# A two-layer decoder trunk on one core: a 128-token linear-attention core, part of the modulation sums taken later, and the first block's expert routing moved behind the first expert layer

## The chip, the core and the metric

The kernel runs on one core of a Trainium2 chip. The core has a matrix engine (PE, TensorE), a vector engine (DVE), a scalar engine (ACT), GpSimd (POOL), which here only gathers rows, and SyncE (SP), which issues almost all other DMAs. Each engine executes its own queue in order. The metric is device time in microseconds (us) of one execution.

## The reference, cut to what matters

512 tokens of width 1024 pass two layers; each layer is an attention and a PEER expert mixer, and each of these is preceded by an RMSNorm with shift and scale and followed by a gate that come from a conditioning vector c.

```python
mod = silu(c) @ mod_w[l] + mod_b[l]              # per layer: sh1, sc1, g1, sh2, sc2, g2, 1024 wide each
# layer 0: gated linear attention, 4 heads, dk 128, dv 256, in chunks of 64 tokens (8 chunks)
b = cumsum(log_a)                                # inside a chunk
scores = tril((q * exp(b)) @ (k * exp(-b)).T);   o = scores @ v + (q * exp(b)) @ state
state = exp(b_last) * state + (k * exp(b_last - b)).T @ v
# layer 1: shared K/V from the output of layer 0, window attention, 16 heads, sinks
# PEER in both layers: q = h @ w_q (8 heads x 2 halves x 128); s = q half @ subkeys (128 keys)
v1,i1 = top_k(s1,16); v2,i2 = top_k(s2,16); cs,ci = top_k(v1[:,None]+v2[None,:],16)
e = i1*128 + i2 of the winners; g = softmax(cs);  y = sum (g * gelu(h . u[e])) * v[e]
```

## The kernel before

Tokens stand in four blocks of 128. Blocks 1 to 3 get the expert mixer densely: `dense` goes over 128 slabs of 128 experts, multiplies every slab with the 384 tokens and weights the result by a routed table. Block 0 gets it by gathering its 128 chosen rows of u and of v per token (`gather_back`), row by row on POOL and DVE while the dense loop of the same layer runs on PE.

**Order of the work.** `gla` first computes norms, projections and decays of all tokens, with PE busy; `gemv` sums modulation vectors beside it: for each of 512 columns (a chunk) four loads of 512 KB, eight DVE operations (L129, L131), and four one-column matmuls (L137). A second loop in `gla` then goes over the four blocks: per head scores (L406), a masked copy (L408), and twice, for either 64-token half, scores times V (L412), q times the state (L413), k times V (L415) and the state's update (L416); then a norm (L148 to L152, L420), the output product with `gla_wo` (L435), and `fin0`, which normalizes the block again and routes it. Routing is `route_front` (four chunks of 32 projection matmuls, L529, with 8 matmul records of key scores, L534, and a top-16 on DVE, L444 to L452), `route` (top-16 of sums, two table lookups, softmax, all DVE) and in `route_block` three transposes (L545). `dense(0)` follows: a prologue writes the routed tables (`routed`, L577 to L591) and computes the first 28 slabs (`act`, L605) ahead; the loop over 128 slabs then does `act` for a later slab (24 matmuls) and 18 matmuls of L639. After the gathered rows of block 0 are summed, `g_attn` does the shared K/V and attention of block 0 and `gather_front` and `gather_sel` route it for layer 1, between the matmuls of the dense loop. `swa_d` ends the dense layer (`dense_end`: gated additions L190, L191, then `modulate_T`), projects K, V and Q (L902), runs window attention per block (`swa_core`), the output product (L916), and routes blocks 1 to 3. `dense(1)` and the end follow.

**What sets the order.** The program is written through a scheduler: each instruction has a priority (lower goes first), `prio(base)` opens a counter at `base`, and an instruction goes into its engine's queue when a time simulation finds its inputs and its buffer ready. The bases are R0 (routing of layer 0), D0 (dense 0), G1 (block 0 in layer 1, just under D0), SW (the window attention stage), R1 (routing of layer 1), D1 and GG (gathers, last). `issue_after(x)` puts an instruction behind x on x's engine. Buffers with one tag are shared: `gw` holds four 4 KB rows on each partition for gathered rows and for `g_attn`'s weights. In `dense` the loads of u (L599), v (L624) and the routed table (L611) go through SP; POOL waits for a free `gw` buffer before each gather (L717).

Of the kernel before, what the change touches and what calls it, by code (L numbers as in the profile page):

```python
# [16 lines left out]
ALU = mybir.AluOpType  # L17
# [25 lines left out]
NA = 28  # L43
GSC = 2.0 ** 14
PACE = [[1.5] * 28 + [2.5] * 100, [1.5] * 28 + [2.25] * 100]
# [3 lines left out]
def kernel(ctx, tc, x, c_col, pos, mod_w, mod_b, norm_g, w_in, w_gl, w_g2, b_g2, gla_ng, gla_wo,  # L49
# [217 lines left out]
    def gla(mod, mod_first, mod_more, finish):  # L267
# [9 lines left out]
        dec = gq.tile([P, HG, S // CH], F32, name="dec")  # L277
# [11 lines left out]
        with tc.tile_pool(name="gla", bufs=1, reuse_waits="tile") as gp1, \  # L289
# [40 lines left out]
            nc.gpsimd.memset(maskf[0:64, 64:128], 0.0)  # L330
# [25 lines left out]
            for h in range(HG):  # L356
# [8 lines left out]
                nc.vector.tensor_copy(dec[:, h, :], az.rearrange("p (c t) -> p c t", t=CH)[:, :, CH - 1])  # L365
# [4 lines left out]
                nc.vector.tensor_tensor(dl, kt_[:, h, :], dl, op=ALU.mult)  # L370
                nc.scalar.activation(bT, bT, AF.Exp, scale=-1.0)
# [17 lines left out]
        with tc.tile_pool(name="gla2", bufs=1, reuse_waits="tile") as g2, \  # L389
# [9 lines left out]
            for half in range(2):  # L399
                bcast_half(env, mod[:, 16:24], half, gate[:, ts(half, 512)])  # L400
            for b in range(NB):
                O = g2.tile([P, D], F32, name="O")
                for h in range(HG):
                    po = ps_tile(env, "po")[:, :DV]
                    psc = mm_tile()
                    nc.tensor.matmul(psc[:, :P], kt_[:, h, ts(b, P)], qt[:, h, ts(b, P)], start=True, stop=True)  # L406
                    sc = scT[h % 2]
                    nc.vector.copy_predicated(sc, mask, psc[:, :P])  # L408
                    for i in range(2):
                        lo = b * P + i * CH  # L410
                        hs = slice(i * CH, (i + 1) * CH)
                        nc.tensor.matmul(po[hs, :], sc[hs, hs], V[hs, b, ts(h, DV)], start=True, stop=False)  # L412
                        nc.tensor.matmul(po[hs, :], qt[:, h, lo:lo + CH], st[:, h, :], start=False, stop=True)  # L413
                        pss = mm_tile()
                        nc.tensor.matmul(pss[:, :DV], kd[hs, b, h, :], V[hs, b, ts(h, DV)], start=True, stop=True)  # L415
                        nc.vector.scalar_tensor_tensor(st[:, h, :], st[:, h, :], dec[:, h, 2 * b + i:2 * b + i + 1],  # L416
                                                       pss[:, :DV], op0=ALU.mult, op1=ALU.add)
# [101 lines left out]
    def route_front(env, l, hT, rp):  # L519
# [3 lines left out]
        for ch in range(4):  # L523
            pq = ps_tile(env, "mm")
            for q in range(4):
                w = wpool.tile([P, KT, P], F32, tag=wtag, name="w", bufs=wbufs)
                nc.sync.dma_start(w, peer_wq[l, ch * 4 + q])
                for kt in range(KT):
                    nc.tensor.matmul(pq[:, ts(q, P)], w[:, kt, :], hT[:, kt, :], start=kt == 0, stop=kt == KT - 1)  # L529
            qq = env.big.tile([P, 512], F32, tag=env.qq, name="qq")  # L530
            nc.scalar.copy(qq, pq)
            psc = ps_tile(env, "sc")
            for q in range(4):
                nc.tensor.matmul(psc[:, ts(q, P)], qq[:, ts(q, P)], sk_sb[l][:, q % 2, :], start=True, stop=True)  # L534
            sc = env.tmp.tile([P, 512], F32, tag=env.t2k, name="scg", bufs=env.scb)
            nc.scalar.copy(sc, psc)
            topk16(rp, [(sc[:, ts(q, P)], v16[:, ch * 4 + q, :], i16[:, ch * 4 + q, :]) for q in range(4)], NK)
        return route(rp, v16, i16)

    def route_block(env, l, b, hT, rp):  # L540
        g, i1, i2 = route_front(env, l, hT, rp)
# [11 lines left out]
    def dense(l, yps):  # L553
        Y = []
        first = []
        wd = dram.tile([NG * P, NK * TG], F32, name=f"wd{l}", tag=f"wd{l}")
        by_slot = wd.rearrange("(g p) (m c) -> m p g c", p=P, c=SL * TG)
        banks = ("y0", "y1", "y2", "y4", "y5", "y3")
        with tc.tile_pool(name="dna", bufs=1, reuse_waits="tile") as da, \
# [84 lines left out]
            with tc.tile_pool(name="dno", bufs=1, reuse_waits="tile") as do_:  # L644
# [3 lines left out]
                for i in range(NG, NA):  # L648
                    act(i, ahead[:, i, :], ("pa", "pm")[i % 2])
# [480 lines left out]
```

## Time and profile before

| | us |
|---|---|
| median of three runs | 3280.8 |
| the three runs | 3267.9 to 3281.03 |
| the profiled execution | 3281.36 |
| its span, first to last instruction | 3279.7 |

| stretch of the span, us | what runs |
|---|---|
| 0 to 222 | norms, projections, decays; modulation sums beside |
| 222 to 432 | linear attention core and output product, block by block; routing begins |
| 432 to 573 | routing of blocks 1 to 3 |
| 573 to 742 | prologue of dense 0 |
| 742 to 1780.5 | loop of dense 0, with gathers, then block 0's layer-1 attention and routing |
| 1780.5 to 2160 | window attention stage and routing of blocks 1 to 3 |
| 2160 to 2310 | prologue of dense 1 |
| 2310 to 3279.7 | loop and end of dense 1 |

The profile is one execution. Busy times are sums over an engine's instructions; a row of a timeline gives start, duration, engine, line, operation, destination and sources with shapes, and in brackets the idle time before it and what ended that. A matmul in plain float32 stands in the trace as two records, so `x64` of L529 is one chunk of 32 matmuls; one in the rounded form of `dense` (L605, L639) is one record.

### The profile page before, as it was taken

To read this page: it belongs to the slowest core of one execution; us is meant where nothing else is said; L and a number is where in the kernel's file an instruction comes from. 1 tells how busy PE (TensorE), PEld (TensorE's weight loads), DVE (VectorE), ACT (ScalarE), POOL (GpSimd) and SP (SyncE) were. 2 spreads that over 40 slices of the span, in tenths; PEclk is the share of its full clock that TensorE was granted. 3 is DMA by queue.
4 is the path that set the end of the run, shared out by engine and by line. 5 is a ranking of instruction groups with operands and counts; after the bars stand their busy time and mean duration, and the time that the engine had idled before them with its cause. 6 is when DMAs were issued, how large, how long until landed. Compare 5 with 4: busy or idle time off the path is not lost.

```text
span 3279.7 us, 45577 instructions
## 1 busy us (share of the span) xinstructions
PE 3087.9 (94%) x16858; PEld 2633.6 (80%) x16858; DVE 2396.3 (73%) x4699; ACT 1282.9 (39%) x1991; POOL 610.3 (19%) x542
## 2 busy tenths in 40 slices
PE   6999985999999999999997889899899999999998
PEld 4765675998889999999876446899789999999997
DVE  7754699989777777777655344999877777777776
ACT  3422322653333333333662344256333333333333
POOL 0000000005333333333000000000433232223230
PEclk9989998999999999999998989999999999999999
DMA  7666675789889898898744225658998888888874
GB/s 238 229 243 237 237 261 169 261 283 345 307 311 317 291 321 311 301 322 287 239 143 145 84 77 193 213 200 294 329 343 311 300 278 305 276 302 303 272 265 154
DMA packets 264888, 844.44 MB, mean 257 GB/s; under 512 B 27844, under 2 KB 77380, under 8 KB 258520
## 3 DMA queue, kind: packets, MB, share of 16 engines
q1 hardware_dynamic: 190936, 573.06, 49.4%
q0 software_dynamic: 73728, 268.47, 24.3%
q8 instruction: 132, 2.16, 0.3%
q14 instruction: 92, 0.75, 0.1%
HBM read 784.27 MB, written 57.16 MB: 257 GB/s over the span
## 4 chain that ended last, share of the span: by engine, by line
PE 81%; DVE 10%; DMA 5%; ACT 2%; issue 1%; SPq 0%; DVEq 0%; ACTq 0%
PE pa L605 32%; PE Y L639 30%; PE ps_mm L529 3%; PE pm L590 3%; PE ps_m L902 2%; DMA v<-in_v_t 1%; PE ps_mm L435 1%; PE ps_mm L260 1%; PE ps_mm L261 1%; PE ps_mm L259 1%; PE ps_mm L916 1%; DMA w<-in_gla_wo 1%; PE ps_po L808 1%; DMA w<-in_mod_w 1%; DVE s L446 1%
## 5 line engine op out<-in xcount | busy, mean ns | idle before, releaser
L717 POOL DMA_INDIRECT gu<-in_peer_u,ei x256 | 314.8, 1230 | 1991.3 <-DVE gu L725 1192.1
L244 DVE TENSOR_TENSOR XL<-u,XH 128x1024 fp32r<-128x1024 f32 x256 | 313.2, 1224 | 351.7 <-PE pa L605 197.4
L639 PE MATMUL Y<-XH,WH 128*128 128x512 f32 x1536 | 480.4, 393 | 9.8 <-ACT WH L243 9.8
L639 PE MATMUL Y<-XH,WL 128*128 128x512 f32 x1536 | 478.5, 393 | 4.1 <-DVE WL L244 4.1
L639 PE MATMUL Y<-XL,WH 128*128 128x512 f32 x1536 | 478.5, 392 | 0.2
L243 ACT CAST XH<-u 128x1024 fp32r<-128x1024 f32 x256 | 269.1, 1052 | 432.1 <-PE pa L605 359.2
L605 PE MATMUL pa<-hH,XH 128*128 128x384 f32 x2048 | 412.4, 341 | 2.2 <-ACT XH L243 1.6
L243 ACT CAST XH<-v 128x1024 fp32r<-128x1024 f32 x256 | 268.8, 1050 | 363.4 <-PE Y L639 312.2
L605 PE MATMUL pa<-hL,XH 128*128 128x384 f32 x2048 | 404.9, 336 | 0.0
L717 POOL DMA_INDIRECT gu<-in_peer_v,ei x256 | 290.9, 1136 | 608.6 <-DVE yg L735 567.4
L605 PE MATMUL pa<-hH,XL 128*128 128x384 f32 x2048 | 401.5, 335 | 2.2 <-DVE XL L244 2.2
L244 DVE TENSOR_TENSOR XL<-v,XH 128x1024 fp32r<-128x1024 f32 x256 | 313.0, 1223 | 109.9 <-ACT XH L243 106.2
L605 PEld LDWEIGHTS pa<-hH,XH 128*128 128x128 f32 x2048 | 365.1, 188 | 20.4 <-ACT XH L243 1.8
L605 PEld LDWEIGHTS pa<-hH,XL 128*128 128x128 f32 x2048 | 358.2, 188 | 3.2 <-DVE XL L244 2.9
L605 PEld LDWEIGHTS pa<-hL,XH 128*128 128x128 f32 x2048 | 358.8, 188 | 1.6 <-issue 0.8
L639 PEld LDWEIGHTS Y<-XH,WL 128*128 128x128 f32 x1536 | 289.0, 188 | 67.4 <-DVE WL L244 5.4
L639 PEld LDWEIGHTS Y<-XL,WH 128*128 128x128 f32 x1536 | 289.0, 189 | 64.4 <-DVE XL L244 1.1
L639 PEld LDWEIGHTS Y<-XH,WH 128*128 128x128 f32 x1536 | 286.3, 189 | 58.3 <-ACT WH L243 11.0
L735 DVE SCALAR_TENSOR_TENSOR yg<-gu,a,yg 128x1024 f32<-128x1024 f32 x254 | 325.0, 1279 | 1.4
L725 DVE SCALAR_TENSOR_TENSOR gu<-gu,htg 128x1024 f32<-128x1024 f32 x256 | 308.4, 1219 | 1.8 <-DMA gu<-in_peer_u,ei 1.7
L243 ACT CAST WH<-g 128x384 fp32r<-128x384 f32 x256 | 131.6, 514 | 383.4 <-DVE g L627 267.5
L529 PE MATMUL ps_mm<-hTd,w 128*128 128x128 f32 x1792 | 223.9, 279 | 10.1 <-DMA w<-in_peer_wq 8.2
(312 smaller groups left out, 3633.1 us busy)
## 6 DMA issues: line engine op xcount, KB each, us to landing
u<-in_u_t SPq DMA_DIRECT2D x256, 512.0 KB, 5.5
v<-in_v_t SPq DMA_DIRECT2D x256, 512.0 KB, 5.2
w<-in_peer_wq SPq DMA_DIRECT2D x128, 512.0 KB, 4.2
w<-in_mod_w SPq DMA_DIRECT2D x96, 512.0 KB, 5.0
wd<-wt SPq DMA_DIRECT2D x48, 1024.0 KB, 6.1
wg<-wd SPq DMA_DIRECT2D x192, 256.0 KB, 9.7
w<-in_gla_wo SPq DMA_DIRECT2D x32, 512.0 KB, 5.0
w<-in_swa_wo SPq DMA_DIRECT2D x32, 512.0 KB, 4.4
```

What stands on the lines that cost most here:

```text
L243: nc.scalar.copy(H, src)
L244: eng.tensor_tensor(L, src, H.bitcast(F32), op=ALU.subtract)
L259: nc.tensor.matmul(out, ah, bh, start=kt == 0, stop=False)
L260: nc.tensor.matmul(out, ah, bl, start=False, stop=False)
L529: nc.tensor.matmul(pq[:, ts(q, P)], w[:, kt, :], hT[:, kt, :], start=kt == 0, stop=kt == KT - 1)
L590: nc.tensor.matmul(pm[:, t, :], o1[:, u, :, w], og[:, n, u, :, w], start=n == 0, stop=n == 1)
L605: nc.tensor.matmul(pa[:, :TD], uu[:, kt, :], hh[:, kt, :], start=n + kt == 0, stop=n == 2 and kt == KT - 1)
L639: nc.tensor.matmul(Y[b][h], a[:, ts(b, P)], vv[:, ts(h, 512)], start=i == 0 and a is WH and vv is VH, stop=i == NK - 1 and a is WL)
L717: nc.gpsimd.indirect_dma_start(out=u, out_offset=None, in_=table, in_offset=bass.IndirectOffsetOnAxis(ap=ei[:, i:i + 1], axis=0))
L725: nc.vector.scalar_tensor_tensor(u, u, 1.0, ht, op0=ALU.mult, op1=ALU.mult, accum_out=a[:, i:i + 1])
L735: nc.vector.scalar_tensor_tensor(y, u, a[:, i:i + 1], y, op0=ALU.mult, op1=ALU.add)
L902: nc.tensor.matmul(pqs[b], hTs[b][:, kt, :], w(kt), start=kt == 0, stop=kt == KT - 1)
```

## The change

Five parts. (1) In `gla` the core works on 128 tokens: the scores of a block are one 128x128 matmul plus one for the 64x64 corner between the halves (from `kx`, a copy of the decayed keys of the first half), the mask keeps the whole lower triangle, q is scaled for the second half once per block (`qs`), and each head then has one q-state matmul, one scores-V, one k-V and one state update. (2) Six of the twelve modulation chunks of layer 1 leave `gla`; `late_mod` sums them inside `gather_back(0)`, from step 40 of the dense loop, two DVE operations per second step, with their loads in `gw` buffers. (3) `route_front` gives its projections, score matmuls and copies a priority of their own (`base`), ahead of the top-16. (4) The layer-1 routing of block 0 leaves the stretch beside dense 0: its first projection chunk is placed behind the last matmul of dense 0, `modulate_T` behind that chunk, the rest into the window attention stage; buffers are listed in another order there, so that the tiles for XD and the weights lie elsewhere. The three transposes of a routed block are placed behind the second projection chunk of the next one. (5) Six `act` slabs of dense 1 go ahead of the routed tables.

```diff
-            nc.gpsimd.memset(maskf[0:64, 64:128], 0.0)
+                even = dl.rearrange("p (b c t) -> p b c t", c=2, t=CH)[:, :, 0, :]
+                nc.scalar.copy(kx[:, h], even)
+                nc.vector.tensor_tensor(even, even, dec[:, h, :, 1:2].to_broadcast([P, NB, CH]), op=ALU.mult)
...
+                nc.scalar.copy(qs[:, :, 0, :], q4[:, :, 0, :])
+                nc.vector.tensor_tensor(qs[:, :, 1, :], q4[:, :, 1, :],
+                                        dec[:, :, b, 0:1].to_broadcast([P, HG, CH]), op=ALU.mult)
...
+                    nc.tensor.matmul(psc[0:CH, CH:P], kx[:, h, b, :], qt[:, h, b * P + CH:(b + 1) * P], start=True,
+                                     stop=True)
                     sc = scT[h % 2]
                     nc.vector.copy_predicated(sc, mask, psc[:, :P])
-                    for i in range(2):
-                        lo = b * P + i * CH
-                        hs = slice(i * CH, (i + 1) * CH)
-                        nc.tensor.matmul(po[hs, :], sc[hs, hs], V[hs, b, ts(h, DV)], start=True, stop=False)
-                        nc.tensor.matmul(po[hs, :], qt[:, h, lo:lo + CH], st[:, h, :], start=False, stop=True)
-                        pss = mm_tile()
-                        nc.tensor.matmul(pss[:, :DV], kd[hs, b, h, :], V[hs, b, ts(h, DV)], start=True, stop=True)
-                        nc.vector.scalar_tensor_tensor(st[:, h, :], st[:, h, :], dec[:, h, 2 * b + i:2 * b + i + 1],
-                                                       pss[:, :DV], op0=ALU.mult, op1=ALU.add)
+                    nc.tensor.matmul(po, qs[:, h].rearrange("p c t -> p (c t)"), st[:, h, :], start=True, stop=False)
+                    nc.tensor.matmul(po, sc, V[:, b, ts(h, DV)], start=False, stop=True)
+                    pss = mm_tile()
+                    nc.tensor.matmul(pss[:, :DV], kd[:, b, h, :], V[:, b, ts(h, DV)], start=True, stop=True)
+                    nc.vector.scalar_tensor_tensor(st[:, h, :], st[:, h, :], decb[:, h, b:b + 1], pss[:, :DV],
+                                                   op0=ALU.mult, op1=ALU.add)
...
+            with prio(base):
+                pq = ps_tile(env, "mm0" if ch == 0 and "mm0" in env.psum else "mm")
...
+            yield mm
...
+                if l:
+                    with prio(R1 - 100_000):
+                        acts(NF)
                 for g in range(NG):
                     routed(g)
-                    act(g, ahead[:, g, :], ("pa", "pm")[g % 2])
+                    acts(max(done, g + 1 if not l else NF + (g + 1) * (NA - NF) // NG))
...
+    def late_mod(at, outs):
+        for n, ch in enumerate(range(6, 12)):
+            acc = gb.tile([P, 512], F32, tag="gacc", name="gacc")
+            for e in range(4):
+                w = gb.tile([P, 2, 512], F32, tag="gw", name="w", bufs=4)
+                nc.sync.dma_start(w, mod_w[1][ch][e // 2, :, 2 * (e % 2):2 * (e % 2) + 2, :])
+                with tc.issue_after(at[LATE + 2 * (4 * n + e)].ins):
...
+            with tc.high_priority(), tc.issue_after(outs[LATE + 8 * n + 9].ins):
...
...
+            for tag, n, bufs in (("Q", 512, 3), ("qT", 512, 3), ("SC", 1024, 4), ("pT", 1024, 4), ("h4k", 1024, 6),
+                                 ("w", 1024, 3), ("mx", 4, 4), ("es", 4, 4), ("nm", 4, 4), ("den", 4, 4)):
                 sp.tile([P, n], F32, tag=tag, name=tag, bufs=bufs)
             XD = xd_tiles(sp)
...
+            renv.psum = {"mm0": (psa, "pm", 1)}
+            sel = gather_sel(renv, 1, hT0, sr, rbase - 600_000)
+            with tc.issue_after(after.ins):
+                first = next(sel)
             preload_sqrt(sp)
+            def after_add(b):
+                with tc.issue_after(first.ins):
+                    modulate_T(env, XD[b], (Ak, Bk, hk[b]), (A, B, hq[b]))
+            dense_end(sp, 0, Y, XD, after_add)
...
+            with prio(rbase - 500_000):
+                sel = rest(sel)
...
+                gen = route_block(renv, 1, b, hT, sr, SW - 100_000)
                 with prio(rbase):
-                    route_block(renv, 1, b, hT, sr)
+                    for _ in range(2):
+                        mm = next(gen)
+                    with tc.issue_after(mm.ins):
+                        rest(tails.pop()) if tails else None
+                    for _ in range(3):
+                        next(gen)
+                tails.append(gen)
...
-            gemv(penv, mod_w[1], range(12), modb_sb[:, 1, :], m1)
+            gemv(penv, mod_w[1], range(6), modb_sb[:, 1, :], m1)
```

## Rows read from the trace of the kernel before

**Rows 1.** The page: busy time of each engine, and the chain's shares.

```profile
PE 3087.9 (94%) x16858; PEld 2633.6 (80%) x16858; DVE 2396.3 (73%) x4699; ACT 1282.9 (39%) x1991; POOL 610.3 (19%) x542
PE 81%; DVE 10%; DMA 5%; ACT 2%; issue 1%; SPq 0%; DVEq 0%; ACTq 0%
```

**Rows 2.** Busy time by stretch: PE, PEld, DVE, ACT, POOL, granted clock, DMA share, GB/s.

```profile
222.00:250.00 28.00, 26.18 (x83) 12.01 (x81) 10.36 (x24) 6.00 (x17) 0.00 (x0) 0.65 0.53 201
372.00:432.00 60.00, 55.16 (x327) 38.74 (x325) 43.91 (x207) 20.92 (x43) 0.00 (x0) 1.00 0.68 233
432.00:573.00 141.00, 97.23 (x801) 92.13 (x801) 128.02 (x738) 32.17 (x50) 3.91 (x4) 0.90 0.61 210
902.00:1230.00 328.00, 327.43 (x1658) 298.03 (x1657) 245.31 (x331) 122.26 (x159) 113.29 (x99) 1.00 0.88 310
1780.50:1807.00 26.50, 0.00 (x0) 0.00 (x0) 25.48 (x123) 9.46 (x10) 3.97 (x4) 0.55 0.47 164
1807.00:1866.00 59.00, 53.48 (x151) 25.25 (x152) 16.58 (x67) 20.78 (x49) 0.96 (x1) 0.94 0.26 91
1866.00:2044.00 178.00, 162.27 (x764) 97.97 (x763) 75.14 (x215) 79.88 (x203) 0.00 (x0) 0.95 0.36 120
2044.00:2160.00 116.00, 100.41 (x769) 96.47 (x768) 107.16 (x642) 39.69 (x52) 0.00 (x0) 0.99 0.59 196
2160.00:2310.00 150.00, 144.01 (x1307) 134.23 (x1305) 138.76 (x125) 84.45 (x146) 0.00 (x0) 1.00 0.74 272
```

**Rows 3.** Timeline of PE in the attention core, blocks 0 to 2.

```profile
233.36 1.11 PE L413 MATMUL ps_po<-st,qt 128*64 128x256 f32 x2
234.40 1.11 PE L412 MATMUL ps_po<-V,scT 64*64 64x256 f32 x2
...
271.52 0.65 PE L413 MATMUL ps_po<-st,qt 128*64 128x256 f32 x2
272.09 0.70 PE L415 MATMUL ps_mm<-V,kd 64*128 64x256 f32 x2
272.72 0.64 PE L412 MATMUL ps_po<-V,scT 64*64 64x256 f32 x2
...
371.74 0.71 PE L415 MATMUL ps_mm<-V,kd 64*128 64x256 f32 x4
```

**Rows 4.** The same timeline in block 3: full-array matmuls, one-column matmuls.

```profile
409.58 3.65 PE L435 MATMUL ps_mm<-w,oT 128*128 128x512 f32 x8
...
424.60 0.95 PE L137 MATMUL ps_tr<-ones,gacc 128*128 128x1 f32 x8
```

**Rows 5.** Stretches of L131 alone: DVE busy (instructions), clock, DMA share, GB/s.

```profile
432.00:573.00 141.00, 14.01 (x19) 0.90 0.61 210
```

**Rows 6.** Waits and DMA issues in 902 to 1240, loop of dense 0.

```profile
POOL gu L717 <- DVE gu L725: 159.8, 59, 7.3
u<-in_u_t SPq DMA_DIRECT2D x41, 512.0 KB, 6.2
```

**Rows 7.** Timeline of SP and ACT in one step of that loop.

```profile
1152.81 0.33 SPq L599 DMA_DIRECT2D u<-in_u_t  x1
1161.58 1.05 ACT L243 CAST XH<-u 128x1024 fp32r<-128x1024 f32 x1 [1.75 <-PE pa L605]
```

**Rows 8.** Timeline at the end of dense 0: PE, SP, DVE, ACT.

```profile
1746.20 7.41 PE L529 MATMUL ps_mm<-hTg,w 128*128 128x128 f32 x64
1754.34 1.16 PE L534 MATMUL ps_sc<-sk,qq 128*128 128x128 f32 x8
1780.89 1.38 SPq L672 DMA_DIRECT2D XD<-xs  x3
1801.18 0.68 DVE L190 TENSOR_TENSOR ga<-Y,gate 128x512 f32<-128x512 f32 x1
1807.06 1.11 PE L163 MATMUL ps_tr<-ident,xn 128*128 128x128 f32 x4 [26.57 <-ACT xn L159]
```

**Rows 9.** Line 605 in 2100 to 2166: ns min/median/max, first and last start.

```profile
L605 PE MATMUL pa<-hH,XH x56: 333/334/537, 2131.2 to 2162.5; 128*128 128x384 f32 x56
```

More of the change, by code (lines that the diff above doesn't have):

```diff
@@ L43 @@
 NA = 28
+NF = 6
 GSC = 2.0 ** 14
+LATE = 40
 PACE = [[1.5] * 28 + [2.5] * 100, [1.5] * 28 + [2.25] * 100]
@@ L703, in gather_sel, with gather_back, extra @@
         return ei, gk
-    def gather_back(l, at, ht, ei, gk):
+    def late_mod(at, outs):
[5 more added lines that the diff above has]
+                with tc.issue_after(at[LATE + 2 * (4 * n + e)].ins):
+                    if e == 0:
+                        nc.vector.tensor_scalar_mul(acc, w[:, 0, :], cs[:, 0:1])
+                    for k in range(e == 0, 2):
+                        nc.vector.scalar_tensor_tensor(acc, w[:, k, :], cs[:, 2 * e + k:2 * e + k + 1], acc, op0=ALU.mult,
+                                                       op1=ALU.add)
+                if e < 3:
+                    yield
+            with tc.high_priority(), tc.issue_after(outs[LATE + 8 * n + 9].ins):
+                col = ps_tile(genv, "tr")
+                for q in range(4):
+                    nc.tensor.matmul(col[:, q:q + 1], acc[:, ts(q, P)], ones1, start=True, stop=True)
+            nc.vector.tensor_tensor(m1[:, ts(ch, 4)], col[:, 0:4], modb_sb[:, 1, ts(ch, 4)], op=ALU.add)
+            if ch == 9:
+                cols["A4"] = mod_scale(m1[:, 32:40], ng_sb[:, 1, 1, :], "A4")
+            yield
+    def gather_back(l, at, outs, ht, ei, gk):
+        more = late_mod(at, outs) if l == 0 else iter(())
+        seen = set()
+        def extra(step):
+            if step >= LATE and step % 2 == 0 and step not in seen:
+                seen.add(step)
+                next(more, None)
         steps = []
@@ L722, in gather_back @@
         for i in range(NH * TOPK):
+            extra(steps[i])
             u = fetch(peer_u, i)
@@ L729, in gather_back @@
         for i in range(NH * TOPK):
+            extra(steps[NH * TOPK + i])
             u = fetch(peer_v, i)
@@ L735, in gather_back @@
                     nc.vector.scalar_tensor_tensor(y, u, a[:, i:i + 1], y, op0=ALU.mult, op1=ALU.add)
+        for _ in more:
+            pass
         gt = row("gt")
@@ L939, in swa_d @@
                         finish(b + 1)
+            with prio(rbase):
+                rest(tails.pop())
+            return sel
     co, sn = rope_tables()
```

115 lines of the change are left out of this document (71 added, 44 removed).

## The prediction

> **What bounds the kernel now.** I read the shares of busy time first, then the busy time by stretch, and only then timelines. PE is busy for 94% of the span and carries 81% of the chain [rows 1], so time comes back where PE idles, where PE does work that could be less, or where another engine holds the end of a stage. The stretches [rows 2] show which is which. In the attention core (222 to 432) PE is the full engine: 26.2 of 28 us in block 0, 55.2 of 60 in block 3, and in block 0 at a granted clock of 0.65, that is with a large part at 1.2 GHz. In 432 to 573 DVE is (128 of 141 us), PE has 44 us idle. In the loop of dense 0 PE idles 0.6 us in 328. Between the dense layers PE idles 26.5 us at a stretch, then 5.5, 15.7 and 15.6 us in three stretches of the attention and routing stage. In the prologue of dense 1 both are near full. All sums are made against the profiled execution, 3281.36 us (span 3279.7 and 1.7 around it); the median, 3280.8, lies 0.6 below.
>
> **1. The core.** Before, a head takes one full score matmul and six matmuls on half of the array. In a warm stretch an L413 holds PE for 0.57 us, and so does an L412; an L415 that stands alone, with 0.70 in its row, holds it for 0.63 [rows 3]. Two L415 next to each other (x4 records) stand there with 0.71 together: those on different halves of the rows do overlap. Of 32 L415 matmuls 10 pairs stand so and 12 alone, 22 x 0.63 = 13.9 us, 0.87 a head. A head costs 4 x 0.57 + 0.87 = 3.15 us beside its full score matmul. After, three full-array matmuls of 256 columns: L435 does 512 columns in 3.65 / 4 = 0.91 us [rows 4], so 0.46 each, 1.37 us; the corner matmul (64 columns, no row of its own) lies between a quarter of 0.46 and a whole half-array step, 0.12 to 0.57; I take 0.35, since it too is on half of the columns. Saved: 3.15 - 1.72 = 1.43 us a head; 12 heads 17.2 us. Block 0's four heads run at steps of 1.04 [rows 3], 1.8 times as long: 4 x 1.43 x 1.8 = 10.3. Together 27.5 us of PE, on the path, because PE is full there. Three of the six chunks that leave lie before 432: 3 x 0.9 us of L137 [rows 4] = 2.7 more. Against it, PE's 4.8 idle us of 60 in block 3 [rows 2], mostly waits for `gla_wo` loads, may grow, and the new copies (`kx`, `qs`, about 0.4 us each on ACT and DVE, which have 65% and 27% of the time free in block 3) can delay a first head: I give back 3. Block 3 is ready 27 us earlier; the bounds are 15 and 36.
> The Trainium skill ("TensorEngine Tiling (Array Packing)", Key Properties) says that different tiles execute weight loads and matmuls in parallel, which speaks against merging halves. The trace agrees for neighbouring L415 [rows 3]; L412 and L413 alternate and don't overlap. If all did, the old head would be as short as the new one and this term would be about 0: a rival below.
>
> **2. Sums that leave the routing tail.** In 432 to 573, 19 of L131 take 14.0 us of DVE [rows 5]; with their first products and additions 15.6. DVE is the full engine there, so the tail shortens by 15.6 to 125 us. Earlier projections (part 3 of the change) can only feed its 13 idle us. Bounds 8 and 28. The start of dense 0 moves by -27 - 15.6, about **-43**.
>
> **3. The sums in dense 0.** 24 one-column matmuls in a full PE: 6 chunks x 0.95 [rows 4] = +6. DVE gets about 36 us over 46 steps; it has a quarter free (245 of 328 [rows 2]). DMA gets 24 loads of 512 KB in 46 x 8.3 = 382 us, 33 GB/s on 310 at a share of 0.88: near full, not over. The point that can go wrong is SP: each load waits there for a `gw` buffer, and behind it stand u, v and table loads. A u load is issued at 1152.81, lands after 6.2 us and is read at 1161.58 [rows 6, 7]: 2.6 us of slack. POOL today waits for such buffers 2.7 us on average [rows 6], about that slack; so I take a few short stalls, +4. Bounds +6 and +25. **+10**.
>
> **4. Block 0's routing out of dense 0.** Four chunks of 7.2 us (the row's 7.41 less the overlap) and 1.1 us of scores [rows 8] leave a full PE: **-33**. `g_attn` itself stays.
>
> **5. The gap.** PE's 26.6 us gap [rows 8] is DVE finishing that routing: the first gated addition starts at 1801.18, 20.7 us after the last matmul, though XD was issued at 1780.89. After, DVE can start at once if XD is loaded early (its tile lies elsewhere), after some 6.5 us if not. From the first addition to the first transpose took 5.9 us. The placed chunk covers 7.4 us; its fourth weight load must wait for a buffer, so I count 8.5 and transposes then: 26.6 - 8.5 = **-18**. Bounds -10 (XD late) and -20. PE no longer stands still before the stage, whose clock is 0.94 and 0.95 [rows 2]; what that gives back is in the next bound.
>
> **6. What the moved work costs there.** Chunks 2 to 4 add 3 x 8.3 = 25 us of PE to a stage with 5.5 + 15.7 us idle up to 2044, in pieces between dependent steps; I let 10 go into idle time: +15. Their 42 us of DVE go into 42 + 103 idle us; each single operation is under 2 us, so the chain is delayed little. The six slabs moved ahead bring less than they look: seven slabs (56 records, 8 each) were already computed from 2131 on, beside the top-16 [rows 9]. They can fill some of the 15.6 us that PE idles in 2044 to 2160, but each costs DVE 1.22 us in a stretch where DVE is at 107 of 116: -5. **+10**, bounds -10 (idle time and clock pay for all) and +31 (nothing is hidden, and the forced order of projections holds up the attention of the next block).
>
> Sum: -43 + 10 - 33 - 18 + 10 = -74; 3281.4 - 74 = **3207**.
>
> **Rivals.** (a) *SP becomes the bound in dense 0*, the case on the slow side: SP waits for each `gw` buffer as long as POOL's longest wait today, 7.3 us [rows 6], instead of the mean. 7.3 - 2.6 = 4.7 us x 24 = 113 us on the PE loop instead of 4: 3207 + 109 = 3316. From 6.5 us of wait per load on (24 x 3.9 = 94 us against 74 + 4 saved, and 16 us for half a percent) the kernel is slower than before. For it: SP's queue is in order. Against it: the scheduler puts a load into the queue when it holds the buffer for free, and the weights of `g_attn` pass SP through `gw` already. 6%. (b) *The core gives nothing*: halves that overlap, or `gla_wo` loads that hold the blocks anyway: only the sums help, -18 instead of -43: 3232. Against it: the steps of 0.57 and 1.04 us [rows 3]. 10%. (c) *The stage takes back what dense 0 gave*: gap -10, moved work +31: 3236. For it: PE is at 90% there. 12%. (d) *All idle time is used*: tail -28, moved work -5: 3180. 7%. (e) *The parts eat each other*, core at its low bound, stalls at +25 and (c) together: about 3265, no change. 5%.
>
> **How the numbers follow.** The forecast, 3207 give or take 22, has 60%. The range that leaves out no more than 2 in 10 goes from just below (d) to above (c): 3165 to 3245. About 0.5%, 16 us, is what a measurement can tell from no change. Faster by more: forecast, b, c, d, 0.89; within: e, 0.05; slower: a, 0.06.
>
> **What would show it.** Right: L412 and L413 at full width, 16 of each, spaced under 0.5 us; the first slab of dense 0 some 43 us earlier; no L131 after the start of the tail; steps of the dense 0 loop still 8.3 us between 40 and 86; the last L639 of dense 0 followed within 1 us by 64 records of L529, and transposes 8 to 9 us behind; the time from that last L639 to the main loop of dense 1 some 8 us shorter than its 530. Wrong: steps of that loop over 8.5 us with SP waiting ahead of u; a DVE that is still full with routing when the core is done, so that the core's gain waits there; an attention stage over 20 us longer behind the transposes.

## The result and the profile after

The changed kernel takes 3245.8 us (median of four, 3238.72 to 3253.74); before, on the same chip, 3280.91 (3267.9 to 3286.62). The ratio is 0.9898, 95% interval 0.9876 to 0.992. The gain is 35 us where 74 were forecast, and the time lies 0.8 us above the top of the range. The profiled execution, 3253.74 us (span 3252.0), is the slowest of the four and gains 27.6; traces are compared on it, and one of the tables below shows how far a first stage moves without any change of its code.

The page of the kernel after, busy time of the engines and the shares of the chain, answers [rows 1]:

```profile
PE 3065.5 (94%) x16794; PEld 2641.4 (81%) x16794; DVE 2392.3 (74%) x4692; ACT 1276.0 (39%) x1997; POOL 628.2 (19%) x541
...
PE 65%; DMA 11%; DVE 10%; issue 8%; POOL 3%; ACT 2%; SPq 0%; POOLq 0%; DVEq 0%; ACTq 0%
```

PE is busy for 22 us less, so most of the 27.6 are work that went; its idle time hardly shrank, 187 us of the span against 192. DMA has 11% of the chain where it had 5%, and "issue" 8% where it had 1%.

Busy time by stretch of the kernel after answers [rows 2] (PE, PEld, DVE, ACT, POOL, granted clock, DMA share, GB/s). The stretches are: routing of blocks 1 to 3, part of the loop of dense 0, the gap, the window stage in four pieces (to the first window scores, to block 1's normalization, to block 3's, to the prologue), the prologue of dense 1.

```profile
386.00:530.00 144.00, 103.23 (x851) 98.25 (x851) 121.26 (x726) 39.86 (x62) 3.91 (x4) 0.90 0.55 187
860.00:1190.00 330.00, 324.14 (x1639) 294.10 (x1638) 256.12 (x357) 115.61 (x155) 122.46 (x94) 0.99 0.91 321
1723.00:1737.30 14.30, 9.00 (x65) 8.81 (x64) 8.38 (x13) 2.60 (x4) 0.00 (x0) 0.84 0.84 339
1737.30:1822.00 84.70, 79.29 (x382) 51.77 (x381) 43.84 (x284) 28.15 (x58) 0.00 (x0) 0.97 0.39 131
1822.00:1920.00 98.00, 84.04 (x348) 44.85 (x347) 51.98 (x124) 40.42 (x110) 3.74 (x4) 0.93 0.27 92
1920.00:2060.00 140.00, 123.89 (x746) 95.38 (x744) 92.48 (x505) 51.16 (x105) 0.00 (x0) 0.90 0.53 177
2060.00:2135.00 75.00, 67.33 (x464) 64.91 (x462) 51.70 (x251) 29.92 (x43) 0.00 (x0) 0.95 0.51 172
2135.00:2283.00 148.00, 138.76 (x1276) 129.36 (x1276) 136.04 (x121) 82.36 (x144) 0.00 (x0) 0.99 0.76 277
```

Two things are new against [rows 2]: the loop of dense 0 has 6 us of PE idle in 330 where it had 0.6 in 328, and the piece 1920 to 2060 has 16 us idle at a clock of 0.90, where [rows 2] have 0.94 to 0.99 in that stage.

**Where the time went.** The table reads each kernel's PE timeline at the same points: the first and the last slab matmul of a dense loop into Y (L639 before, L658 after), the first transposes behind dense 0, the first slab matmul of dense 1's loop. All in us; the experiments' rows are used further down.

| kernel | loop of dense 0 starts | loop | gap | first transposes to dense 1's loop | loop of dense 1 |
|---|---|---|---|---|---|
| before | 742.7 | 1037.8 | 26.6 | 505.6 | 951.9 |
| after | 698.7 | 1024.4 | 14.2 | 545.8 | 954.2 |
| change | -44.0 | -13.4 | -12.4 | +40.2 | +2.3 |
| forecast | -43 | -33 + 10 | -18 | +10 | 0 |
| e3, core alone | 714.0 | 1038.9 | 26.6 | 510.7 | 950.5 |
| e2, sums back in the prologue | 716.0 | 999.4 | 12.1 | 546.4 | 953.2 |
| e5, late sums without loads | 700.7 | 1009.2 | 13.4 | 547.6 | 951.7 |
| g1, loads issued by POOL | 707.8 | 1020.7 | 14.2 | 545.5 | 952.4 |
| g2, a quarter of the bytes | 705.4 | 1012.9 | 14.0 | 545.6 | 951.7 |
| e4, block 0 back in dense 0 | 705.6 | 1051.8 | 26.6 | 520.4 | 953.4 |
| e1, projections behind attention | 706.3 | 1020.4 | 14.9 | 530.6 | 951.4 |
| e6, no early slabs | 702.4 | 1021.6 | 14.0 | 544.8 | 952.6 |
| f1, e1 and e2 | 709.0 | 999.5 | 12.8 | 532.4 | 954.0 |
| f2, f1 with free transposes | 714.5 | 1000.8 | 5.2 | 536.1 | 952.2 |
| g3, block 0 behind first scores | 712.4 | 999.8 | 5.2 | 546.6 | 950.7 |

The changes add to -27.3. Against the forecast 9.6 us are missing in the loop, 5.6 in the gap and 30.2 in the window stage; the first stage came as forecast, within its noise. The first column shows that noise: e2, f1, f2 and g3 run the same code up to there and start dense 0 at 709.0 to 716.0; the kernel after, e5, g1, g2, e4, e1 and e6 do so too and start it at 698.7 to 707.8, the kernel after first of all. Differences under some 9 us in that column say nothing, and the mean of those seven, 703.8, lies 38.9 ahead of the kernel before. In the other columns equal code agrees within 5 (505.6 and 510.7 in before and e3).

### The profile page after: what moved, and what is told of

It reads as the page before. It is cut to its first block, busy times and chain, and to the rows that moved or that the text cites. A ratio compares the mean times of both kernels' runs of the same rounds, so it can differ in the third digit from the quotient of the medians.

```text
span 3252.0 us, 45442 instructions
## 1 busy us (share of the span) xinstructions
PE 3065.5 (94%) x16794; PEld 2641.4 (81%) x16794; DVE 2392.3 (74%) x4692; ACT 1276.0 (39%) x1997; POOL 628.2 (19%) x541
## 4 chain that ended last, share of the span: by engine, by line
PE 65%; DMA 11%; DVE 10%; issue 8%; POOL 3%; ACT 2%; SPq 0%; POOLq 0%; DVEq 0%; ACTq 0%
PE pa L624 24%; PE Y L658 22%; PE ps_mm L543 6%; POOL gu L786 3%; DMA gu<-in_peer_v,ei 3%; PE pm L609 3%; DMA w<-in_mod_w 2%; PE ps_m L995 2%; DMA v<-in_v_t 1%; DVE XL L246 1%; DVE gacc L133 1%; PE ps_mm L1009 1%; PE ps_po L881 1%; DMA u<-in_u_t 1%; PE ps_mm L262 1%
## 5 line engine op out<-in xcount | busy, mean ns | idle before, releaser
L786 POOL DMA_INDIRECT gu<-in_peer_u,ei x256 | 325.0, 1269 | 1947.0 <-DVE gu L795 1209.8
L246 DVE TENSOR_TENSOR XL<-u,XH 128x1024 fp32r<-128x1024 f32 x256 | 312.8, 1222 | 297.1 <-PE pa L624 164.4
L658 PE MATMUL Y<-XH,WH 128*128 128x512 f32 x1536 | 481.0, 393 | 11.1 <-ACT WH L245 11.1
L658 PE MATMUL Y<-XH,WL 128*128 128x512 f32 x1536 | 478.9, 393 | 4.8 <-DVE WL L246 4.8
L658 PE MATMUL Y<-XL,WH 128*128 128x512 f32 x1536 | 478.6, 392 | 0.2
L245 ACT CAST XH<-u 128x1024 fp32r<-128x1024 f32 x256 | 269.1, 1052 | 467.9 <-PE pa L624 299.7
L786 POOL DMA_INDIRECT gu<-in_peer_v,ei x256 | 298.8, 1167 | 607.7 <-DVE yg L806 536.9
L245 ACT CAST XH<-v 128x1024 fp32r<-128x1024 f32 x256 | 268.7, 1050 | 302.9 <-PE Y L658 258.4
L246 DVE TENSOR_TENSOR XL<-v,XH 128x1024 fp32r<-128x1024 f32 x256 | 312.6, 1221 | 96.5 <-ACT XH L245 90.4
L658 PEld LDWEIGHTS Y<-XH,WL 128*128 128x128 f32 x1536 | 289.0, 189 | 69.1 <-DVE WL L246 6.9
L658 PEld LDWEIGHTS Y<-XL,WH 128*128 128x128 f32 x1536 | 289.3, 189 | 64.9 <-DVE XL L246 1.1
L658 PEld LDWEIGHTS Y<-XH,WH 128*128 128x128 f32 x1536 | 286.6, 189 | 59.9 <-ACT WH L245 12.2
L245 ACT CAST WH<-g 128x384 fp32r<-128x384 f32 x256 | 131.6, 514 | 441.7 <-DVE g L646 322.9
L543 PE MATMUL ps_mm<-hTd,w 128*128 128x128 f32 x1792 | 223.7, 284 | 8.8 <-ACT hTd L173 5.1
```

Of the source, the lines that this page charges most:

```text
L245: nc.scalar.copy(H, src)
L246: eng.tensor_tensor(L, src, H.bitcast(F32), op=ALU.subtract)
L543: mm = nc.tensor.matmul(pq[:, ts(q, P)], w[:, kt, :], hT[:, kt, :], start=kt == 0, stop=kt == KT - 1)
L658: mm = nc.tensor.matmul(Y[b][h], a[:, ts(b, P)], vv[:, ts(h, 512)], start=i == 0 and a is WH and vv is VH, stop=i == NK - 1 and a is WL)
L786: nc.gpsimd.indirect_dma_start(out=u, out_offset=None, in_=table, in_offset=bass.IndirectOffsetOnAxis(ap=ei[:, i:i + 1], axis=0))
```

## The experiments

Two disputes were open: what lengthens the loop of dense 0 when the late sums are in it, and what lengthens the window stage.

**e3: the core alone**, the kernel before with part 1 of the change.

```diff
+                    nc.tensor.matmul(psc[0:CH, CH:P], kx[:, h, b, :], qt[:, h, b * P + CH:(b + 1) * P], start=True, stop=True)
...
-                    for i in range(2):
...
+                    nc.tensor.matmul(po, qs[:, h].rearrange("p c t -> p (c t)"), st[:, h, :], start=True, stop=False)
+                    nc.tensor.matmul(po, sc, V[:, b, ts(h, DV)], start=False, stop=True)
...
```

> The kernel before with the 128-token core alone. Predicted for the core: block 3 27 us earlier, all of it reaching dense 0 since the routing tail keeps its length: 3281 - 27 = 3254. Rival: the routing of the four blocks on DVE is what ends the stage, so that an earlier core only meets a longer tail: less than 12 us, 3270. In the changed kernel core and sums together moved dense 0 by 44 us; the core alone shows how they share it.

Measured: 3254.53 us, ratio 0.9897 (0.9864 to 0.993); dense 0 starts 28.7 us earlier. The term of 27 stands. The ratio is that of the whole change, but its interval is wide; in medians the core alone gains 28.4 us (from 3282.88) and the whole change 35.1. PE's timeline of the kernel after in the core, warm blocks:

```profile
314.86 0.60 PE L427 MATMUL ps_mm<-V,kd 128*128 128x256 f32 x2
315.29 0.59 PE L424 MATMUL ps_po<-st,qs 128*128 128x256 f32 x2
315.72 0.59 PE L425 MATMUL ps_po<-V,scT 128*128 128x256 f32 x2
...
336.37 0.38 PE L419 MATMUL ps_mm<-qt,kt__187 128*128 128x128 f32 x2
336.68 0.33 PE L420 MATMUL ps_mm<-qt,kx 128*64 128x64 f32 x2
336.94 0.94 PE L551 MATMUL ps_sc<-sk,qq 128*128 128x128 f32 x6
```

A full-width step is 0.43 us (forecast 0.46) and the corner matmul, which had no row before, 0.26 (forecast 0.35). Against the halves' 0.57 [rows 3], merging pays, and the run shows that the alternating halves of this core did not run side by side. "TensorEngine Tiling (Array Packing)", Key Properties, of the Trainium skill speaks against this term only in the point that the prediction took, that different tiles work in parallel. The point ahead of it in the same list says that a change of the tiling mode drains TensorE, and L412 (64x64) and L413 (128x64) are of different modes; so the list as a whole does not make this term 0. Whether a drain is what kept them apart no run here shows.

**e2: the sums back in the prologue**, the kernel after without part 2.

```diff
-            gemv(penv, mod_w[1], range(6), modb_sb[:, 1, :], m1)
+            gemv(penv, mod_w[1], range(12), modb_sb[:, 1, :], m1)
...
-        more = late_mod(at, outs) if l == 0 else iter(())
+        more = iter(())
...
```

> The changed kernel with the six modulation chunks back in the first stage; nothing is summed beside the loop of dense 0. If the sums behave as predicted, the start of dense 0 moves 15 to 18 us later and dense 0 gets 10 shorter: 3252. If the loads and sums cost the loop of dense 0 about 20 us, as its 10 us of idle PE and six us of one-column matmuls suggest (with slower steps besides), the two cancel: 3242 to 3248, dense 0 back at 1005 us from its first to its last matmul of Y, against 1024 after and 1038 before with 33 us of block 0's projections in it.

Measured: 3242.93, ratio 0.9861 (0.9828 to 0.9895). The loop of dense 0 becomes 25 us shorter, and dense 0 starts later: 17 us against the one run after, 9 between the means of the five kernels with the sums in the prologue (713.2) and the seven without (703.8). So moving the sums costs about 22 (mean loop 1022 in after, e1, e6 and g1 against 999.9 in e2, f1, f2 and g3) and gains 9 to 17: it is a loss of some 5 to 13 us by the traces. The medians of after and e2, 2.9 us apart with intervals that overlap, are too close to show it alone; the same edit between e1 and f1 (below) is worth 11.3 in median. The runs of those two do not overlap, but they come from two chips, and the intervals of their ratios do overlap.

**e5: the late sums without their loads**, and so without the `gw` buffers that these take; the sums' DVE and PE work is done on a tile that is there already.

```diff
-                w = gb.tile([P, 2, 512], F32, tag="gw", name="w", bufs=4)
-                nc.sync.dma_start(w, mod_w[1][ch][e // 2, :, 2 * (e % 2):2 * (e % 2) + 2, :])
+                w = hH.rearrange("p k t -> p (k t)")[:, 0:1024].bitcast(F32).rearrange("p (k c) -> p k c", c=512)
```

> The changed kernel, its late sums read a resident tile instead of the loaded weights: 24 loads of 512 KB and their buffers leave the loop of dense 0, the DVE operations and the one-column matmuls stay; the sums are of wrong numbers. Dense 0, from its first to its last Y matmul, took 1024 us with the sums and 999 in e2 without. Theory L (the loads: SP's order, the shared buffers, the DMA engines): 1005 to 1009, the six us of one-column matmuls and little more. Rival C (DVE and PE work): 1018 or more.

**g1: the same loads issued by POOL.**

```diff
-                nc.sync.dma_start(w, mod_w[1][ch][e // 2, :, 2 * (e % 2):2 * (e % 2) + 2, :])
+                nc.gpsimd.dma_start(w, mod_w[1][ch][e // 2, :, 2 * (e % 2):2 * (e % 2) + 2, :])
```

> The changed kernel with the 24 loads of the late sums issued by POOL, which issues the gathers, instead of SP. The loads cost the loop of dense 0 about 13 to 15 us (1009 us without them in e5, 1022 on average with them). Theory S (SP's order): a load that waits on SP for its buffer, or takes SP's place, delays the u loads behind it; from POOL it can't, and the loop falls to 1007 to 1013. Rival B (buffers and DMA engines): the loop stays at 1019 or more, whoever issues them.

**g2: a quarter of the bytes**, same count of loads, same buffers, same queue.

```diff
-                nc.sync.dma_start(w, mod_w[1][ch][e // 2, :, 2 * (e % 2):2 * (e % 2) + 2, :])
+                wl = gb.tile([P, 2, 512], F32, tag="gw", name="w", bufs=4)
+                nc.sync.dma_start(wl[:, 0:1, 0:256], mod_w[1][ch][e // 2, :, 2 * (e % 2):2 * (e % 2) + 1, 0:256])
+                w = hH.rearrange("p k t -> p (k t)")[:, 0:1024].bitcast(F32).rearrange("p (k c) -> p k c", c=512)
...
```

> The changed kernel whose 24 late loads bring 128 KB instead of 512 KB, into the same buffers, from SP, at the same places; the sums read a resident tile and take a scalar from the loaded one, so DVE and PE do the same work and each buffer is held as long; the sums are of wrong numbers. If bytes count (DMA share 0.91 in that loop, u landing after 7.0 us instead of 6.2), most of the 13 to 15 us go: 1012 or less. If the wait for a shared buffer in SP's order counts, or rows that come late because a buffer is taken, the loop stays at 1018 to 1024.

Measured, one profiled run each: 3239.06 us (e5), 3257.03 (g1), 3245.99 (g2). The loop is 1009.2, 1020.7 and 1012.9 against 1024.4 after and about 1000 without late sums. Busy time in 410 us of the loop, starting 165 us behind its first slab (columns as above), kernel after:

```profile
864.00:1274.00 410.00, 403.24 (x2038) 364.99 (x2038) 322.05 (x429) 141.99 (x191) 154.79 (x118) 1.00 0.90 319
```

The same of e5:

```profile
866.00:1276.00 410.00, 410.00 (x2089) 373.89 (x2088) 331.19 (x438) 151.08 (x196) 149.13 (x123) 1.00 0.87 307
```

The same of g1:

```profile
873.00:1283.00 410.00, 404.09 (x2041) 366.77 (x2040) 322.17 (x427) 143.03 (x191) 164.61 (x140) 0.99 0.91 321
```

The same of g2:

```profile
870.00:1280.00 410.00, 407.80 (x2071) 369.98 (x2070) 326.37 (x434) 144.34 (x194) 157.09 (x119) 1.00 0.89 307
```

Waits in the same stretch of the kernel after (us in total, times, longest): ACT, which converts each slab of u, for u's load.

```profile
ACT XH L245 <- DMA u<-in_u_t: 85.7, 28, 7.0
```

The same wait in e5:

```profile
ACT XH L245 <- DMA u<-in_u_t: 23.1, 9, 4.2
```

The same wait in g2 (in g1 it is 94.3 us):

```profile
ACT XH L245 <- DMA u<-in_u_t: 86.6, 29, 6.1
```

DMA issues there, kernel after, u's loads (count, size, median us from issue to landing):

```profile
u<-in_u_t SPq DMA_DIRECT2D x47, 512.0 KB, 7.0
```

The same of e5:

```profile
u<-in_u_t SPq DMA_DIRECT2D x49, 512.0 KB, 5.4
```

PE is full in e5 and loses 6.8 us in this stretch after, 5.9 in g1, 2.2 in g2. So of the 22 us that the late sums put into the loop, about 9 are the sums' own work (e5 against e2; the six chunks of one-column matmuls were priced at 6), and 13 are the loads together with the `gw` buffers that they hold, since e5 takes out both. SP's order, the reason that the prediction named, is not it: taken off SP they cost the same (g1). Nor does a load of u stand behind others on SP: in all four kernels SP issues it, in the median, 0.03 us after its buffer has come free, and 0.1 to 0.2 us on average.

With a quarter of the bytes about 9 of the 13 are gone, yet ACT still waits 86.6 us for u, as long as after. The shared buffers make u late, whatever the bytes. POOL waits for `gw` buffers that the sums hold, so gathered rows come late, and DVE, which takes them in the order of its queue, stands for them. Two of these waits, kernel after:

```profile
POOL gu L786 <- DVE gacc L753: 34.3, 15, 4.4
DVE yg L806 <- DMA gu<-in_peer_v,ei: 24.9, 15, 5.1
```

The same two in g2:

```profile
POOL gu L787 <- DVE gacc L754: 32.6, 14, 4.0
DVE yg L807 <- DMA gu<-in_peer_v,ei: 19.2, 15, 3.0
```

With the same wait for the gathered rows of u, DVE stands 49.5 us after, 43.3 in g1, 42.9 in g2, and not at all in e5 and e2. Every slab of u or v is split in two: ACT makes the high half XH (L245), then DVE the low half XL (L246). A load of u takes the buffer of an earlier slab of v, which comes free when DVE has made that slab's XL. DVE starts on it a median 2.5 us behind the end of ACT's half after and in g2, 2.2 in g1, 0.6 in e5. The longest stall of the stretch after shows the whole way, from DVE's wait for a gathered row to PE:

```profile
1125.41 1.28 DVE L806 SCALAR_TENSOR_TENSOR yg<-gu,a,yg 128x1024 f32<-128x1024 f32 x1 [2.94 <-DMA gu<-in_peer_v,ei]
1126.62 1.22 DVE L246 TENSOR_TENSOR XL<-v,XH 128x1024 fp32r<-128x1024 f32 x1
...
1127.86 0.34 SPq L618 DMA_DIRECT2D u<-in_u_t  x1
...
1137.89 1.04 ACT L245 CAST XH<-u 128x1024 fp32r<-128x1024 f32 x1 [6.96 <-DMA u<-in_u_t]
...
1139.38 1.01 PE L624 MATMUL pa<-hH,XH 128*128 128x384 f32 x2 [4.31 <-ACT g L626]
```

ACT's `g`, for which PE stalls, stands in ACT's queue behind the conversion that waits for u. All five stalls of PE over 0.1 us in this stretch, and all four in g1, follow such a wait; the longest waits for u are 7.0 us after, 8.6 in g1, 6.1 in g2 and 4.2 in e5. So with the buffers shared, bytes carry most of the price that reaches PE. What is left without them, about 4 us in one run each, is no more than the loops of after, e1, e6 and g1 differ among themselves. Whether full loads in buffers of their own would cost anything, no run here shows.

The rates fit this and do not prove it: in e5 u, v, table and gathers take 307 GB/s, the sums' loads would add the forecast's 33, and after moves 319. "DMA: Bandwidth & Descriptors", Specifications, of the Trainium skill gives about 358 GB/s of HBM to a core. The means of the stretches shown here stay below it, but the highest of the 10 us slices of this stretch after moves 390 GB/s, so in this run the figure is no ceiling. The page's section "Issuing engines are not separate DMA queues" says that DMAs run on the same 16 engines whoever issues them; g1 agrees (1020.7 for 1024.4).

**e4: block 0's routing back beside dense 0**, without the chunk placed behind its end.

```diff
-            sel = gather_sel(renv, 1, hT0, sr, rbase - 600_000)
-            with tc.issue_after(after.ins):
-                first = next(sel)
...
-            with prio(rbase - 500_000):
-                sel = rest(sel)
...
+            gs.append((ht, *rest(gather_sel(genv, 1, hT0, gf, G1 + 200_000))))
...
```

> The changed kernel with the layer-1 routing of block 0 back beside the end of dense 0, and no order forced between its projections and the normalizations behind dense 0; buffers as in the changed kernel. Predicted price of moving it: -33 in dense 0, -18 in the gap, +15 behind. The traces of the two kernels say -33, -12 and +28 to +30. By the prediction this run takes 3246 + 36 = 3282; by the traces 3246 + 16 = 3262. If XD is loaded early whatever is routed when, part of the gap stays closed and it takes less than 3262 only if the gap came from XD and not from the routing on DVE.

Measured: 3268.37, ratio 0.9955 (0.9939 to 0.9972). Loop and gap come back (1051.8, 26.6). But the window stage stays at 520.4, 14.8 longer than before and 9.7 longer than in e3, with none of block 0's routing in it.

**e1: the projections of blocks 1 to 3 in layer 1 behind the attention**, one base changed.

```diff
-                gen = route_block(renv, 1, b, hT, sr, SW - 100_000)
+                gen = route_block(renv, 1, b, hT, sr, rbase - 200_000)
```

> The changed kernel with one thing undone: in the window attention stage the projections of blocks 1 to 3 get a priority behind attention again (still ahead of the top-16). Theory O (order): the projections that stand as whole blocks of 35 us in PE's queue ahead of the next block's attention hold back blocks 2 and 3 (their last normalization comes 336 us after dense 0 instead of 259), and DVE lacks routing work meanwhile; undone, the stage gets about 14 us shorter (8 to 30): 3232, and block 3 is ready less than 300 us after dense 0. Rival W (work): PE is full in that stage whatever the order, and only the 25 us of block 0's projections count; then the time stays at 3246 give or take 5.

Measured: 3237.69, ratio 0.9849 (0.9813 to 0.9884). The window stage falls from 545.8 to 530.6. The two experiments undo different halves and agree: the order +14.8 (e4 against before; +9.7 against e3) or +15.2 (after against e1), block 0's routing +25.0 (e1 against before; +20 against e3). The normalization of blocks 1, 2, 3 (first and last start of the row) and the projections of their routing, kernel after and then e1, 1800 to 2100:

```profile
L161 ACT ACTIVATE xn<-XD,rs x3: 1146/1148/1150, 1918.4 to 2057.9; 128x1024 f32<-128x1024 f32 x3
...
L543 PE MATMUL ps_mm<-hTd,w x768: 274/275/582, 1921.5 to 2098.0; 128*128 128x128 f32 x192
```

```profile
L161 ACT ACTIVATE xn<-XD,rs x3: 1148/1149/1149, 1921.3 to 1997.2; 128x1024 f32<-128x1024 f32 x3
...
L543 PE MATMUL ps_mm<-hTd,w x768: 272/275/582, 1924.3 to 2086.8; 128*128 128x128 f32 x192
```

Block 1 is as early in both. Block 3 is ready 139.5 us later after, 75.9 in e1. The 41 us behind block 1's normalization show what PE does instead, kernel after and then e1: all of PE's work, then L543 alone (PE, PEld, clock, DMA share, GB/s).

```profile
1920.00:1961.00 41.00, 39.24 (x288) 36.18 (x287) 18.59 (x105) 14.03 (x37) 0.00 (x0) 0.88 0.51 173
...
1920.00:1961.00 41.00, 31.77 (x243) 31.19 (x244) 0.88 0.51 173
```

```profile
1923.00:1964.00 41.00, 39.00 (x194) 25.33 (x193) 12.18 (x24) 20.28 (x48) 0.00 (x0) 0.95 0.50 167
...
1923.00:1964.00 41.00, 12.53 (x82) 11.10 (x82) 0.95 0.50 167
```

PE is equally busy. After spends 31.8 of 39.2 us on projections, at a clock of 0.88; e1 spends 12.5 of 39.0 on them and the rest on other work, the attention of the next block among it, at 0.95. Block 3's routing ends last, so projections of block 1 that push it back by 64 us are early work on the wrong block; the shorter rest behind it gets 49 of the 64 back.

**e6: no slabs of dense 1 ahead of the routed tables.**

```diff
-                if l:
-                    with prio(R1 - 100_000):
-                        acts(NF)
...
-                    acts(max(done, g + 1 if not l else NF + (g + 1) * (NA - NF) // NG))
+                    acts(g + 1)
```

> The changed kernel without the six slabs put ahead of the routed tables in dense 1. Predicted for them: 5 us. In both traces the first slab starts 33 us before the last routing transposes and the prologue takes 148 us, so I now expect no more than 3 us of difference from the dense end to the loop of dense 1, which was 560 us. If they help by filling PE beside the routing, that time grows by 5 to 20 us.

Measured in one profiled run: 3251.78 us; the stage is 544.8 against 545.8. The early slabs move nothing that can be told from noise.

**f1: e1 and e2 together.**

```diff
...
+                gen = route_block(renv, 1, b, hT, sr, rbase - 200_000)
...
+            gemv(penv, mod_w[1], range(12), modb_sb[:, 1, :], m1)
...
```

> The changed kernel with both found losses undone: projections of blocks 1 to 3 behind attention (as in e1) and the six modulation chunks back in the first stage (as in e2). If both losses are separate, as their stages are, they add: from e2's dense end at 1715 and e1's 546 us from there to the loop of dense 1, the run takes 1715 + 546 + 954 + 2, with the end behind the last matmul, about 3229 by the clock of those runs, some 14 us below e2. If the 14 us of e1 came from the sums' traffic in some way, f1 is no better than e2 or e1, 3238 to 3243.

Measured: 3226.42 (3220.59 to 3230.96), before 3282.22, ratio 0.9835 (0.9815 to 0.9854). This beats both kernels: core, block 0's routing out of the loop, the placed chunk, and neither late sums nor early projections in layer 1.

**f2: f1 with the first transposes not forced behind the placed chunk.**

```diff
-                with tc.issue_after(first.ins):
-                    modulate_T(env, XD[b], (Ak, Bk, hk[b]), (A, B, hq[b]))
+                modulate_T(env, XD[b], (Ak, Bk, hk[b]), (A, B, hq[b]))
```

> f1 without the order that puts the normalizations behind the whole first projection chunk. In the changed kernel the gap behind dense 0 was 14.2 us: three quarters of the chunk done after 5.5 us, then 5.3 us of PE waiting for the fourth weight load, while the first block's normalized rows were there at 8.1. If that forced order is what holds the gap, it falls to 8 or 9 us and the kernel is 5 us faster than f1. If PE's work in the stage is what counts, the gap falls but the first scores of the attention come at the same time, and nothing is gained.

The gap in the kernel after, timeline of all engines:

```profile
1722.48 0.62 PE L658 MATMUL Y<-XH,WL 128*128 128x512 f32 x2
1722.67 1.39 SPq L119 DMA_DIRECT2D w<-in_kv_w  x3
1722.93 5.52 PE L543 MATMUL ps_mm<-hTg,w 128*128 128x128 f32 x48
...
1724.75 0.69 DVE L192 TENSOR_TENSOR ga<-Y,gate 128x512 f32<-128x512 f32 x1 [7.60 <-DMA gate<-grow]
1724.91 12.98 SPq L541 DMA_DIRECT2D w<-in_peer_wq  x4
...
1730.00 1.15 ACT L161 ACTIVATE xn<-XD,rs 128x1024 f32<-128x1024 f32 x1 [0.23 <-DVE rs L154]
...
1733.75 3.78 PE L543 MATMUL ps_mm<-hTg,w 128*128 128x128 f32 x16 [5.30 <-DMA w<-in_peer_wq]
...
1737.32 1.06 PE L165 MATMUL ps_tr<-ident,xn 128*128 128x128 f32 x4
```

The placed chunk covers 5.5 us, then PE stands 5.3 us for its fourth weight load, and the transposes must stand behind it though `xn` is made at 1731. In f2, PE's timeline at the same place, they go ahead of it:

```profile
1715.15 5.52 PE L543 MATMUL ps_mm<-hTg,w 128*128 128x128 f32 x48
1720.50 0.60 PE L165 MATMUL ps_tr<-ident,xn 128*128 128x128 f32 x4
```

Measured: gap 5.2 against 12.8. But the rest of that chunk is still to be done, the stage behind is 536.1 for 532.4, and the whole, 3229.29 with ratio 0.9847 (0.9825 to 0.9869), can't be told from f1.

**g3: f2 with the rest of block 0's routing behind the first half of block 1's window attention** (its scores and their products with V).

```diff
...
-            with prio(rbase - 500_000):
-                sel = rest(sel)
...
+                    if kp == 0 and b == 0:
+                        with prio(rbase - 500_000), tc.issue_after(mm.ins):
+                            sel = rest(sel)
```

> f2 with the second to fourth projection chunk of block 0 placed behind the attention of the first block, where PE idles (14 us of 98 in the changed kernel), instead of between the K, V and Q projections, where it is full. If the place is why the 25 us of this work hid nothing, the stage from the dense end to the loop of dense 1, 541 us in f2, falls by 8 to 15. If PE's idle time there is made of short waits inside dependent chains that other work doesn't fill, the work costs its 25 us wherever it stands: within 4 us of f2.

Busy time in f2 and then g3, from the first transposes to the first window scores, and on to block 1's normalization (columns as above):

```profile
1720.50:1805.80 85.30, 78.33 (x393) 51.22 (x391) 44.85 (x284) 28.09 (x58) 0.00 (x0) 1.00 0.46 151
1805.80:1904.70 98.90, 84.93 (x350) 45.24 (x349) 53.24 (x127) 40.11 (x110) 3.75 (x4) 0.93 0.27 91
```

```profile
1717.40:1774.80 57.40, 53.15 (x167) 25.83 (x165) 15.32 (x63) 20.94 (x49) 0.00 (x0) 0.97 0.32 108
1774.80:1913.40 138.60, 112.34 (x576) 71.94 (x575) 81.93 (x346) 47.66 (x120) 3.75 (x4) 0.91 0.35 113
```

Measured: 3234.73, ratio 0.9856 (0.9824 to 0.9888). The 28 us leave the piece ahead of the scores and come back in the next one with 12 more: PE idles 14 us there in f2 and 26 in g3. That block 0's chunks stand ahead of the scores is not why they hid nothing.

## Why the prediction was right or wrong

**The core (step 1): right.** -27 forecast, -28.7 alone.

**The sums out of the tail (step 2): right within the noise**, 15.6 forecast, 9 to 17 measured. The two steps together gave -44.0 for -43; that it is so near is in part luck, since by the mean of the seven kernels with the same first stage it is -38.9.

**The sums in dense 0 (step 3): mis-sized, and the reason was wrong.** Forecast 10, measured about 22, inside the bounds of 6 and 25. With block 0's routing still in the loop the sums add only 13 to 14 (1051.8 in e4 against 1038.9 in e3 and 1037.8 before), so the price of this step hangs on step 4. The work was 9 for 6, near enough. The stalls were priced at 4 with SP as the suspect; the loads and their buffers cost 13, and SP has no part in it. The step asked who waits for a `gw` buffer at SP alone. POOL's gathers wait for the same buffers, DVE waits for the gathers, and DVE frees the buffers of u; this chain was not in the prediction. DMA was called "near full, not over" and given nothing, but with these buffers shared, three quarters of the bytes are 9 of the 13. u's landing, 5.4 us without these loads (e5; 6.2 before), is 7.0 with them, out of a slack that the same paragraph had put at 2.6. Rival (a) rested on the same suspect and falls with it.

**Block 0 out of dense 0 (step 4): right.** -33 forecast; -39 where no late sums stand (1038.9 in e3 to 999.9), -30 where they do (1051.8 in e4 to 1022).

**The gap (step 5): mis-sized.** -18 forecast, -12.4 measured, inside the bounds. The chunk's fourth weight load was counted as a wait, but only up to 8.5 us; it landed later, and the transposes are placed behind it. f2 shows a gap of 5.2 with the placing gone, which is worth little because the work only moves.

**The moved work (step 6): the step that failed.** +10 forecast, +40 measured, above its upper bound of 31. Three terms in it: block 0's 25 us of chunks were to hide 10 and hid 0 to 5 (e1 +25 or +20); the early slabs were to give 5 and gave nothing (e6); and the early priority of the projections in layer 1, 15 us, was not priced. The step counts PE's idle 5.5 + 15.7 us as room. Ahead of the first window scores PE is busy for 53.5 of 59 us before [rows 2] and for 79.3 of 84.7 after: 26 us more work in a piece that is 26 us longer, and the idle 5 us stay. These are pieces between dependent steps on a PE that is 90% busy, and work put there comes back nearly in full (e1) or with more (g3). Part 3 of the change was costed only in layer 0, in step 2, where e3 without it and the kernels with it start dense 0 alike (714.0 against 713 on average); in layer 1 it stood only as half a sentence under a bound, and that bound was too low for both at once. Rival (c), 3236, named the place, with the gap at -10 and the stage at +31, and comes nearest. Its nearness is in part luck: the profiled execution lies 17.7 us above it, with 9.6 of them in the loop and 9.2 in the stage, and the median happens to lie 8 below that execution.

Of the signs named for right, steps under 0.5 us, the earlier first slab and no sums in the routing tail came true. Four did not: steps 40 to 86 of the dense 0 loop take 8.73 us on average where they took 8.31 before, 17 of them over 8.5; behind the last L658 stand 48 records of L543 at once and not 64, and the transposes 14.2 us behind it and not 8 to 9; and the time from there to dense 1's loop is 28 us longer, not 8 shorter. Of the signs named for wrong, steps over 8.5 us came, though SP was not what held u back, and the attention stage over 20 us longer came in full.

## What to carry to other kernels

Idle time that a profile shows in pieces between dependent steps is no room for moved work: on a stage that is 90% busy count the moved work in full until a run shows otherwise. When a change raises a priority, ask which block ends last and whether that block gets earlier; early work for another block is a delay. When new loads share buffers with others, ask which engine waits for those others and what it frees: here the late buffer was paid by POOL, DVE and ACT before PE stalled. With buffers shared like this, bytes added at a DMA share of 0.88 were a cost, whoever issued them.

## What the runs showed of the hardware

The late sums' 24 loads of 512 KB with their shared buffers (after against e5) raised the DMA share of the dense loop only from 0.87 to 0.90 and the rate from 307 to 319 GB/s, but the waits for u from 23.1 to 85.7 us and PE's idle time in 410 us from 0 to 6.8. The waits are not a matter of the rate: in g2, at 307 GB/s, they are 86.6. Slices of 10 us of that loop moved up to 390 GB/s. The granted clock of a PE that was equally busy in both kernels, 39 us of 41, was 0.88 while mostly 128-column projections ran and 0.95 while other work had two thirds of it. Both lie between its two levels, 1.2 and 2.4 GHz. The clock may be a part of the 15 us that the order costs; how large a part no run here separates.
